# A hybrid attention, S5 and RG-LRU step: score and gate products over 128 rows, sample PV in two runs

## The chip, the cores and the metric

The kernel runs on one core of a Trainium2 chip. The metric is device time in microseconds of one execution. TensorE (PE in the profile) multiplies matrices into PSUM; VectorE (DVE), ScalarE (ACT) and GpSimd (POOL) do the elementwise work; SyncE (SP) issues most of the DMAs.

## The reference

One layer over a prompt of 2048 tokens and eight sample sequences of 4 tokens each (2080 token columns), in f32. `proj = x @ w_in` (1024 to 6400 columns) is split into queries, keys, values, gates and the inputs of three branches:

- attention with a window of 128 keys, 8 query heads of 64 in 2 groups of keys and values, a relative bias and a sink per head: `scores = q k^T / 8 + bias`, softmax with the sink in the denominator, times v. The sample sequences attend to 128 cached keys and their own.
- S5, a diagonal complex state space with a GELU and a gated output.
- RG-LRU: `r = sigmoid(x_block @ w_a + b_a)`, `i = sigmoid(x_block @ w_x + b_x)` for eight blocks of 64, then a linear recurrence.

Each branch is multiplied by its gate and by its `w_branch`; the three are merged with sigmoid gates, multiplied by `w_out`, added to the scaled input and normalised. The states and caches are returned too.

## The kernel before

Products are made accurate by splitting a number into a high part, which the fast matmul type float32r holds, and a low part. `mm3` (lines 98 to 101) adds three matmuls: high by high, high weights by low input, low weights by high input.

The first phase is `x @ w_in`: 48 column tiles of 128, each over five token units of 512, 512, 512, 272 and 272 columns (`gemm`, 24 matmuls a unit). Side streams for S5, its GLU, RG-LRU and attention are Python generators; `tick` counts the columns issued so far and takes a step of the current stream after so many, so the order of all instructions is fixed when the program is built. The second phase multiplies the three branches (`y_unit`), the third is `w_out` and the layer norm.

Units of the gate tiles are evacuated by one ScalarE and two VectorE operations (L89, L104, L233), the other units of attention's time by ScalarE alone.

RG-LRU (`lru_stream`): 4 column blocks by 5 chunks (512, 512, 512, 284, 284 columns). `f_split` makes for each half g a tile `f` whose own 64 rows hold that half's high part and whose other 64 rows its low part. Four matmuls a chunk write the PSUM tile `sa`: high weights by all 128 rows of `f` (L887), then low weights by the own 64 rows (L890). The weights `lru_w` stand in both halves of the rows.

Attention (`attn_stream`): 16 blocks of 128 queries, two groups, so 32 scores. `score(n)` has eight matmuls in four pairs:

```python
PE.matmul(o, hi.rearrange("p i t -> p (i t)"), kk[kv][:, keys], start=True, stop=False)
PE.matmul(o, lo.rearrange("p i t -> p (i t)"), kl[rows, keys], start=False, stop=True)
```

The first (L1024) has queries with high and low parts stacked over 128 rows, against the keys' high part in both halves; the second (L1025) the queries' high part, 64 rows, against the keys' low part `kl`. Columns are 192 (64 and 128 in block 0). An iteration n issues `score(n)`, the copies of the next block's queries and keys (`prep`), PV of score n-2 (`pvm`, L1099), the four transposes of the weights of score n-1 (`ptr`, L1051), VectorE's addition of the bias and the maximum (L1039 on), and, after 2.5 units of x @ w_in, the exponentials (ScalarE, L89) and the normalisation (VectorE, L1008 to L1010). The transposes of the next iteration need the last of these. `vtr` transposes a block's values (L982) from the tile `vr`.

The sample sequences come after the prompt's attention. Their PV (L1227, L1228) has for each of eight sequences a product over 128 cached rows and one over 4 new rows, plain f32, each of which shows as two matmuls in the trace.

Of the kernel before, what the change touches and what calls it, by code (L numbers as in the profile page):

```python
# [27 lines left out]
# how much of x @ w_in runs between the steps of a side stream  # L28
# [5 lines left out]
# column tiles of w_in in the order of the first phase  # L34
# [19 lines left out]
def kernel(ctx: ExitStack, tc: tile.TileContext, I, O):  # L54
# [81 lines left out]
    # ------------------------------------------------------------ side streams  # L136
    # A stream yields how much of x @ w_in its engines need before its next step.
# [19 lines left out]
    # ------------------------------------------------------------ weight stream  # L157
# [25 lines left out]
    # ------------------------------------------------------------ evacuations of the first phase  # L183
# [52 lines left out]
    # ------------------------------------------------------------ S5  # L236
    def s5_stream():
# [18 lines left out]
        # relative bias along the distance, for the attention's table  # L256
# [70 lines left out]
        # powers of the transition, 0..8  # L327
# [16 lines left out]
        # input matrix  # L344
# [24 lines left out]
        # per group with real over imaginary: powers for the output kernel, and the fourth for the samples  # L369
# [10 lines left out]
        # decay over eight steps and its unit phase, whose powers undo the rotation  # L380
# [61 lines left out]
        # lag kernels, with d at lag nought  # L442
# [217 lines left out]
        # final states  # L660
# [15 lines left out]
    # ------------------------------------------------------------ S5: GELU and GLU  # L676
# [73 lines left out]
    # ------------------------------------------------------------ RG-LRU  # L750
# [6 lines left out]
    def lru_stream():  # L757
# [9 lines left out]
        # log sigmoid  # L767
# [49 lines left out]
        def x_in(i, c):  # L817
            """Inputs of a chunk with the three before; the samples follow with their own."""
            t0, n = LUN[c]
            x = p.tile([128, 516], FT, name=uid("lx"), tag="lx", bufs=2)  # L820
            if c == 0:
                G.memset(x[:, 0:3], 0.0)
                SD.dma_start(x[:, 3:3 + n], xD[i][:, :n])
            else:
                m = min(t0 + n, TP) - t0 + 3
                SD.dma_start(x[:, :m], xD[i][:, t0 - 3:t0 - 3 + m])
            if c == 4:
                SD.dma_start(O["conv_p"][:, i], x[:, 228:231])
                smp = x[:, 231:287].rearrange("p (b s) -> p b s", s=7)
                V.tensor_copy(smp[:, :, 0:3], c0[:, i])  # L830
                SD.dma_start(smp[:, :, 3:7], xD[i][:, TP:T].rearrange("p (b t) -> p b t", t=4))
                SD.dma_start(O["conv_s"][:, i], smp[:, :, 4:7])
            cin[i, c] = x
# [19 lines left out]
        def f_split(j):  # L853
            """A block's values with high and low parts stacked; its own half is high."""
            if j >= len(chunks):
                return
            i, c = chunks[j]
            t0, n = LUN[c]
            o = xfs[i][:, t0:t0 + n]
            fs = [p.tile([128, 512], FR, name=uid("f"), tag=f"f{g}")[:, :n] for g in range(2)]  # L860
            for g in range(2):
                own, oth = half(g)
                act(fs[g][own], o[own], AF.Copy)
                V.tensor_sub(fs[g][oth], o[own], fs[g][own])
            return fs
# [15 lines left out]
        for i in range(4):  # L881
            wh, wl = wt
            R = big("R")
            for c, (t0, n) in enumerate(LUN):
                ps = sa()
                for g in range(2):
                    PE.matmul(ps[:, g, :n], wh[:, g], cur[g], start=True, stop=False)  # L887
                for g in range(2):
                    own = half(g)[0]
                    PE.matmul(ps[:, g, :n], wl[own, g], cur[g][own], start=False, stop=True)  # L890
                cur = f_split(i * 5 + c + 1)
                xf = xfs[i]
                ig = p.tile([128, 512], FT, name=uid("ig"), tag="ig")
                for g in range(2):
                    own, oth = half(g)
                    act(R[own, t0:t0 + n], ps[own, g, :n], AF.Tanh, scale=0.5, bias=hba[own, i:i + 1])
                    act(ig[own, :n], ps[oth, g, :n], AF.Tanh, scale=0.5, bias=hbx[oth, i:i + 1])
                stt(xf[:, t0:t0 + n], ig[:, :n], 1.0, xf[:, t0:t0 + n], OP.add, OP.mult)
                conv(i * 5 + c + 2)
                if c == 2 and i + 1 < 4:  # L900
                    wt = w_prep(i + 1)
                    w_in_(i + 2)
                yield
            b_ = xf
            aa = big("a")
            act(aa, R, AF.Exp, scale=c2[:, i:i + 1], bias=c2[:, i:i + 1])
            yield
            act(R, R, AF.Tanh, scale=nc2[:, i:i + 1], bias=nc2[:, i:i + 1])
            yield
            act(R, R, AF.Sqrt)  # L910
            stt(R, aa, 1.0, R, OP.add, OP.mult)
            stt(b_, b_, 0.5, R, OP.mult, OP.mult)
            V.memset(aa[:, 2048:2104].rearrange("p (b s) -> p b s", s=7)[:, :, 2], 0.0)
            V.tensor_copy(b_[:, 2048:2104].rearrange("p (b s) -> p b s", s=7)[:, :, 2], l0[:, i])
            V.tensor_tensor_scan(R, aa, b_, 0.0, op0=OP.mult, op1=OP.add)
            hs = p.tile([128, 8, 4], FT, name=uid("hs"), tag="hs", bufs=2)
            V.tensor_copy(hs, R[:, 2048:2104].rearrange("p (b s) -> p b s", s=7)[:, :, 3:7])
            SD.dma_start(hD[i][:, :TP], R[:, :TP])
            SD.dma_start(hD[i][:, TP:T], hs.rearrange("p b t -> p (b t)"))
            SD.dma_start(O["lru_p"][:, i:i + 1], R[:, 2047:2048])  # L920
            SD.dma_start(O["lru_s"][:, i], hs[:, :, 3])
            yield
            if i + 1 < 4:
                yield
        es.close()

    # ------------------------------------------------------------ attention
    def attn_stream():
# [5 lines left out]
        # Partitions hold 64 queries of two heads: the first or the second half of a block, with the 192 keys  # L934
        # that this half may see. A query's bias runs over the same distances in either half.
# [5 lines left out]
        raw, QK, ST_, VN = {}, {}, {}, {}  # L941

# [3 lines left out]
        def load(b):  # L946
# [5 lines left out]
            v = w([128, 128], "vr", bufs=3)  # L952
# [3 lines left out]
        def prep(b):  # L956
            q, k, v = raw.pop(b)
            k0 = 0 if b else 128
            # a group's queries with high and low parts stacked, its keys' high part twice; the group's own half is high
            qs = [w([128, 2, 4, 64], f"q{g}", FR) for g in range(2)]  # L960
            kk = [w([128, 256], f"k{g}", FR) for g in range(2)]
            kl = w([128, 256], "kl", FR)
# [6 lines left out]
            QK[b] = (qs, kk, kl, v)  # L969

            def low():
                for g in range(2):
# [3 lines left out]
                    V.tensor_sub(kl[own, k0:], k[own, k0:], kk[g][own, k0:])  # L976
# [3 lines left out]
        def vtr(b):  # L980
            ps = psum.tile([128, 512], FT, name=uid("mm"), tag="mm", bufs=3)
            PE.transpose(ps[:, 0:128], QK[b][3], ident)  # L982
# [3 lines left out]
            # the rows' halves as they are, the first twice, the second twice, swapped  # L986
# [8 lines left out]
        def soft_max(P, m, nh, sinks_ap):  # L995
            """P: scores [128, nh, n], replaced by the weights of the softmax; m: its sums."""
# [15 lines left out]
        def score(n):  # L1012
            b, kv = divmod(n, 2)
            qs, kk, kl, _ = QK[b]
            rows = slice(kv * 64, kv * 64 + 64)
# [3 lines left out]
            for h in range(2):  # L1019
                keys = slice(64 * h + k0[h], 64 * h + 192)  # L1020
                for i in range(2):
                    o = pv[:, h, i, k0[h]:]
                    hi, lo = qs[kv][:, h, 2 * i:2 * i + 2], qs[kv][rows, h, 2 * i:2 * i + 2]
                    PE.matmul(o, hi.rearrange("p i t -> p (i t)"), kk[kv][:, keys], start=True, stop=False)  # L1024
                    PE.matmul(o, lo.rearrange("p i t -> p (i t)"), kl[rows, keys], start=False, stop=True)  # L1025
# [6 lines left out]
            def front():  # L1032
# [7 lines left out]
                # of the outer 64 keys on either side, a query sees each in one block only  # L1040
# [107 lines left out]
        # ---- the sample group: all sequences at once, keys of the others left out  # L1148
# [25 lines left out]
        # cache rows that stay, then the new rows behind them  # L1174
# [50 lines left out]
        for b_ in range(8):  # L1225
            c = slice(b_ * 16, b_ * 16 + 16)
            PE.matmul(pv[:, :, b_], vc[:, b_], PT[:, :, c], start=True, stop=False)  # L1227
            PE.matmul(pv[:, :, b_], vnn[:, b_], PN[:, :, c], start=False, stop=True)  # L1228
# [8 lines left out]
    # ------------------------------------------------------------ first phase: x @ w_in  # L1237
# [41 lines left out]
    # ------------------------------------------------------------ inputs of the second phase  # L1279
# [56 lines left out]
    def seam(ti, u):  # L1336
        """Steps among the last units of the first phase that bring the second one's first inputs."""
# [83 lines left out]
    # ------------------------------------------------------------ second phase: branches, token units inside  # L1421
# [50 lines left out]
    def out_mm(t):  # L1472
# [4 lines left out]
        # the last tile in narrower column groups, whose statistics run while the next one is formed  # L1477
# [40 lines left out]
    # branch units; the next branch's inputs follow the last use of their place  # L1518
# [145 lines left out]
```

## Time and profile before

| | us |
|---|---|
| three runs | 1840.19, 1844.46, 1844.7 |
| median | 1844.46 |
| profiled execution: span | 1842.3 |
| TensorE busy | 1826.7 (99%) |
| TensorE weight loads busy | 1563.8 (85%) |
| VectorE busy | 1130.6 (61%) |
| ScalarE busy | 654.9 (36%) |
| GpSimd busy | 167.5 (9%) |

Of the profiled execution the page gives its span, from the first to the last instruction; what a run takes beside it is not listed apart. Busy times are shares of that span. Records of TensorE overlap, because a matmul is still running when the next one starts, so a mean duration is not a price: the distance between starts is. The granted clock is 1.00 at 2.4 GHz and 0.50 at 1.2 GHz.

### The profile page before, as it was taken

The numbers are of one execution on the slowest core, as the hardware profiler recorded it, in microseconds if no ns is written. First come the engines' busy times: TensorE is split into PE (matmuls) and PEld (weight loads), VectorE is DVE, ScalarE is ACT, GpSimd is POOL, SyncE is SP. The second block draws the span as 40 slices with busy tenths as digits, with TensorE's granted clock in tenths as the row PEclk, the third lists the DMA queues.
The fourth block names the chain that finished last, engine by engine and source line by source line (L and its number), as shares of the span: only waits on it lengthen the run. The fifth ranks groups of instructions, "written<-read, shape, count | busy, mean of one in ns | idle before, by whom it ended". The sixth has DMA issues, their size and how long they took to land. (4 is left out here: it accounts for less than half of the span.)

```text
span 1842.3 us, 26628 instructions
## 1 busy us (share of the span) xinstructions
PE 1826.7 (99%) x9788; PEld 1563.8 (85%) x9788; DVE 1130.6 (61%) x2450; ACT 654.9 (36%) x1382; POOL 167.5 (9%) x375
## 2 busy tenths in 40 slices
PE   8999999999999999999999999999999999999998
PEld 7888888888899888888888888888888888888886
DVE  5765888884343565544666788744343567666666
ACT  6213344432433466764455555411220202111110
POOL 0000000000000000000345454500000000000000
PEclk9999999999999999999999999999999999999999
DMA  7443343343333344343322334353454646542222
GB/s 229 111 130 102 115 115 106 108 114 109 113 112 100 95 124 108 92 102 103 96 79 75 104 105 124 101 164 97 140 171 140 195 131 197 181 147 91 92 91 75
DMA packets 214038, 220.36 MB, mean 120 GB/s; under 512 B 89124, under 2 KB 156708, under 8 KB 212740
## 3 DMA queue, kind: packets, MB, share of 16 engines
q1 hardware_dynamic: 182532, 169.27, 32.3%
q10 hardware_dynamic: 31376, 49.39, 7.5%
q8 instruction: 77, 1.26, 0.3%
q14 instruction: 53, 0.43, 0.1%
HBM read 136.53 MB, written 83.14 MB: 119 GB/s over the span
## 5 line engine op out<-in xcount | busy, mean ns | idle before, releaser
L99 PE MATMUL mm<-xh,wh 128*128 128x512 f32 (+1 forms) x1920 | 681.2, 355 | 0.0
L101 PE MATMUL mm<-xh,wl 128*128 128x512 f32 (+1 forms) x1920 | 673.8, 351 | 0.0
L100 PE MATMUL mm<-xl,wh 128*128 128x512 f32 (+1 forms) x1920 | 671.8, 350 | 0.0
L99 PEld LDWEIGHTS mm<-xh,wh 128*128 128x128 f32 x1920 | 362.0, 189 | 47.4 <-issue 2.9
L101 PEld LDWEIGHTS mm<-xh,wl 128*128 128x128 f32 x1920 | 361.6, 188 | 46.9 <-DVE wl L94 0.3
L100 PEld LDWEIGHTS mm<-xl,wh 128*128 128x128 f32 x1920 | 362.2, 189 | 42.2
L99 PE MATMUL py<-ah,wbh 128*128 128x512 f32 (+1 forms) x480 | 169.0, 352 | 1.2 <-DVE acc L104 1.2
L101 PE MATMUL py<-ah,wbl 128*128 128x512 f32 (+1 forms) x480 | 168.9, 352 | 0.0
L100 PE MATMUL py<-ah,wbh 128*128 128x512 f32 (+1 forms) x480 | 168.8, 352 | 0.0
L89 ACT ACTIVATE st<-mm 128x512 f32<-128x512 f32 (+1 forms) x170 | 86.9, 511 | 168.1 <-PE mm L101 154.5
L99 PEld LDWEIGHTS py<-ah,wbh 128*128 128x128 f32 x480 | 90.2, 188 | 14.6 <-issue 1.6
L100 PEld LDWEIGHTS py<-ah,wbh 128*128 128x128 f32 x480 | 90.3, 188 | 12.8
L101 PEld LDWEIGHTS py<-ah,wbl 128*128 128x128 f32 x480 | 90.2, 188 | 12.5
L1488 PE MATMUL po<-woh,mh 128*128 128x512 f32 x224 | 88.8, 396 | 0.0
L1490 PE MATMUL po<-woh,ml 128*128 128x512 f32 x224 | 88.8, 396 | 0.0
L1489 PE MATMUL po<-wol,mh 128*128 128x512 f32 x224 | 88.8, 396 | 0.0
L94 DVE TENSOR_TENSOR wl<-wr,wh 128x1024 fp32r<-128x1024 f32 x48 | 59.3, 1236 | 40.9 <-ACT wh L89 40.9
L104 DVE SCALAR_TENSOR_TENSOR gt<-gt,mm 128x512 f32<-128x512 f32 (+1 forms) x60 | 35.0, 584 | 72.5 <-ACT gt L89 72.3
L104 DVE SCALAR_TENSOR_TENSOR br<-br,py 128x512 f32<-128x512 f32 (+1 forms) x80 | 46.8, 585 | 50.9 <-PE py L101 43.7
L89 ACT ACTIVATE gt<-mm 128x512 f32<-128x512 f32 (+1 forms) x60 | 30.9, 516 | 120.6 <-PE mm L101 120.2
L89 ACT ACTIVATE wbh<-wbr 128x512 fp32r<-128x512 f32 x24 | 15.1, 629 | 148.0 <-PE py L100 117.3
L89 ACT ACTIVATE wh<-wr 128x1024 fp32r<-128x1024 f32 x48 | 50.5, 1051 | 23.7 <-DMA wr<-in_w_in_dram 10.0
(346 smaller groups left out, 2761.9 us busy)
## 6 DMA issues: line engine op xcount, KB each, us to landing
wr<-in_w_in_dram SPq DMA_DIRECT2D x48, 512.0 KB
mD<-st ACTq DMA_DIRECT2D x72, 256.0 KB
br<-mD SPq DMA_DIRECT2D x71, 256.0 KB
lx<-in_xr_dram SPq DMA_DIRECT2D x16, 512.0 KB
mD<-st ACTq DMA_DIRECT2D x48, 136.0 KB
br<-mD SPq DMA_DIRECT2D x47, 136.0 KB
xr<-in_xT_dram SPq DMA_DIRECT2D x24, 256.0 KB
wbr<-in_w_br_dram SPq DMA_DIRECT2D x24, 256.0 KB
```

Of the source, the lines that this page charges most:

```text
L89: return A.activation(out, in_, func, bias=bias, scale=scale, **kw)
L94: V.tensor_sub(lo, src, hi)
L99: PE.matmul(ps, wh, xh, start=start, stop=False)
L100: PE.matmul(ps, wh, xl, start=False, stop=False)
L101: PE.matmul(ps, wl, xh, start=False, stop=stop)
L104: return (eng or V).scalar_tensor_tensor(out, a, s, b, op0=op0, op1=op1)
L1488: PE.matmul(ps[c], h[:, k, :rows], wh, start=k == 0, stop=False)
L1489: PE.matmul(ps[c], h[:, k, :rows], wl, start=False, stop=False)
L1490: PE.matmul(ps[c], l[:, k, :rows], wh, start=False, stop=k == 7)
```

## The change

In RG-LRU the low weights are multiplied by all 128 rows of `f` instead of its own 64. In attention the keys' low part gets a tile for each group, whose other 64 rows are set to nought once, and the second product of a pair uses the same 128-row queries as the first. The value tile `vr` has two places instead of three. The sample PV issues the eight 128-row products first and then the eight 4-row ones, all into one PSUM bank, with one start and one stop. Comments were taken out, which shifts lines by a few.

```diff
                 for g in range(2):
-                    own = half(g)[0]
-                    PE.matmul(ps[:, g, :n], wl[own, g], cur[g][own], start=False, stop=True)
+                    PE.matmul(ps[:, g, :n], wl[:, g], cur[g], start=False, stop=True)
...
+        kl = [p.tile([128, 256], FR, name=f"kl{g}") for g in range(2)]
+        for g in range(2):
+            G.memset(kl[g][half(g)[1]].bitcast(FT), 0.0)
...
-            v = w([128, 128], "vr", bufs=3)
+            v = w([128, 128], "vr", bufs=2)
...
-            kl = w([128, 256], "kl", FR)
...
-            QK[b] = (qs, kk, kl, v)
+            QK[b] = (qs, kk, v)
...
-                    V.tensor_sub(kl[own, k0:], k[own, k0:], kk[g][own, k0:])
+                    V.tensor_sub(kl[g][own, k0:], k[own, k0:], kk[g][own, k0:])
...
-                    hi, lo = qs[kv][:, h, 2 * i:2 * i + 2], qs[kv][rows, h, 2 * i:2 * i + 2]
-                    PE.matmul(o, hi.rearrange("p i t -> p (i t)"), kk[kv][:, keys], start=True, stop=False)
-                    PE.matmul(o, lo.rearrange("p i t -> p (i t)"), kl[rows, keys], start=False, stop=True)
+                    qq = qs[kv][:, h, 2 * i:2 * i + 2].rearrange("p i t -> p (i t)")
+                    PE.matmul(o, qq, kk[kv][:, keys], start=True, stop=False)
+                    PE.matmul(o, qq, kl[kv][:, keys], start=False, stop=True)
...
         for b_ in range(8):
             c = slice(b_ * 16, b_ * 16 + 16)
-            PE.matmul(pv[:, :, b_], vc[:, b_], PT[:, :, c], start=True, stop=False)
-            PE.matmul(pv[:, :, b_], vnn[:, b_], PN[:, :, c], start=False, stop=True)
+            PE.matmul(pv[:, :, b_], vc[:, b_], PT[:, :, c], start=b_ == 0, stop=False, skip_group_check=True)
+        for b_ in range(8):
+            c = slice(b_ * 16, b_ * 16 + 16)
+            PE.matmul(pv[:, :, b_], vnn[:, b_], PN[:, :, c], start=False, stop=b_ == 7, skip_group_check=True)
```

## Rows read from the trace of the kernel before

**Rows 1.** The page's busy time of each engine (share of the span), with its instructions.

```profile
PE 1826.7 (99%) x9788; PEld 1563.8 (85%) x9788; DVE 1130.6 (61%) x2450; ACT 654.9 (36%) x1382; POOL 167.5 (9%) x375
```

**Rows 2.** Waits of TensorE, whole span: total us, times, longest; first and last.

```profile
PE mm L99 <- ACT xh L89: 4.9, 1, 4.9
...
PE mm L100 <- DVE xl L94: 0.2, 1, 0.2
```

**Rows 3.** Timeline of TensorE, an RG-LRU chunk of 512 columns: start, us, instruction.

```profile
627.04 0.40 PE L101 MATMUL mm<-xh,wl 128*128 128x512 f32 x1
627.27 0.63 PE L887 MATMUL sa<-f,lwh 128*128 128x512 f32 x2
...
628.59 0.40 PE L100 MATMUL mm<-xl,wh 128*128 128x512 f32 x1
```

**Rows 4.** Timeline of TensorE, a score and the PV behind it.

```profile
990.45 0.25 PE L1024 MATMUL sa<-k,q 128*128 128x192 f32 x1
990.63 0.35 PE L1025 MATMUL sa<-kl,q 64*128 64x192 f32 x1
990.91 0.36 PE L1024 MATMUL sa<-k,q 128*128 128x192 f32 x1
...
992.85 0.28 PE L1099 MATMUL sb<-ptl,vn 128*128 128x256 f32 x1
992.96 0.28 PE L1099 MATMUL sb<-ptq,vn 128*128 128x256 f32 x1
```

**Rows 5.** Timeline of TensorE: four transposes of a score, and that of block 13's values.

```profile
1128.92 0.60 PE L1051 MATMUL sc<-ident,S 128*128 128x128 f32 x4
...
1132.39 0.27 PE L982 MATMUL mm<-ident,vr 128*128 128x128 f32 x1
```

**Rows 6.** Timeline of TensorE's weight loads, in the score of rows 4.

```profile
990.91 0.19 PEld L1024 LDWEIGHTS sa<-k,q 128*128 128x128 f32 x1
...
992.85 0.19 PEld L1099 LDWEIGHTS sb<-ptq,vn 128*128 128x128 f32 x1
```

**Rows 7.** Groups by line and shape: busy us, mean ns, idle before.

```profile
L890 PE MATMUL sa<-f,lwl 64*128 64x512 f32 x24 | 6.0, 496 | 0.0
```

**Rows 8.** Timeline of TensorE, an RG-LRU chunk of 284 columns.

```profile
646.19 0.43 PE L887 MATMUL sa<-f,lwh 128*128 128x284 f32 x2
...
647.21 0.40 PE L100 MATMUL mm<-xl,wh 128*128 128x512 f32 x1
```

**Rows 9.** Timeline of TensorE, the sample PV and x @ w_in behind it.

```profile
1274.43 0.31 PE L1227 MATMUL sc<-PT,vc 128*128 128x32 f32 x2
...
1275.00 0.41 PE L1227 MATMUL sc<-PT,vc 128*128 128x32 f32 x2
...
1275.67 0.41 PE L1227 MATMUL sc<-PT,vc 128*128 128x32 f32 x2
...
1281.43 0.63 PE L100 MATMUL mm<-xl,wh 128*128 128x512 f32 x1
...
1284.84 0.40 PE L99 MATMUL mm<-xh,wh 128*128 128x512 f32 x1
```

**Rows 10.** Stretches: length, busy us (instructions) of each engine, granted clock, DMA.

```profile
1278.04:1284.84 6.80, 6.80 (x20) 5.62 (x20) 1.23 (x1) 1.60 (x3) 0.00 (x0) 0.50 0.06 10
...
876.45:1043.17 166.72, 166.72 (x888) 138.24 (x887) 112.52 (x245) 88.33 (x270) 77.58 (x154) 1.00 0.27 86
1043.17:1178.39 135.22, 135.22 (x723) 112.18 (x721) 113.83 (x239) 69.12 (x217) 66.11 (x129) 1.00 0.36 111
```

**Rows 11.** Timeline of GpSimd, its first work in attention, with the idle time before.

```profile
864.39 0.61 POOL L989 CAST vn<-vn 64x512 fp32r<-64x512 f32 x1 [116.30 <-DMA mD<-st]
```

**Rows 12.** Timeline of SyncE's queue: the load of block 15's values.

```profile
1146.76 0.38 SPq L953 DMA_DIRECT2D vr<-vD  x1
```

**Rows 13.** Waits of VectorE from 876 to 1043, then 1043 to 1178 us.

```profile
DVE S L1039 <- PE sa L1025: 36.6, 16, 3.9
...
DVE S L1039 <- PE sa L1025: 10.0, 7, 2.2
```

**Rows 14.** Timeline of VectorE, the normalisation before the transposes of rows 5.

```profile
1127.25 0.69 DVE L1010 TENSOR_TENSOR S<-S,m 128x512 f32<-128x512 f32 x1
```

More of the change, by code (lines that the diff above doesn't have):

```diff
@@ L981, in vtr @@
             ps = psum.tile([128, 512], FT, name=uid("mm"), tag="mm", bufs=3)
-            PE.transpose(ps[:, 0:128], QK[b][3], ident)
+            PE.transpose(ps[:, 0:128], QK[b][2], ident)
             h = w([128, 4, 2, 2, 64], "vn", FR, 3)
@@ L1013, in score @@
             b, kv = divmod(n, 2)
-            qs, kk, kl, _ = QK[b]
-            rows = slice(kv * 64, kv * 64 + 64)
+            qs, kk, _ = QK[b]
             ps = sa()
```

## Prediction

> **What bounds the kernel now.** The page comes first. TensorE is busy for 1826.7 of 1842.3 us, 99% of the span, and VectorE for 61% [rows 1]. The waits of TensorE come next: the first and the last of the five rows are 4.9 and 0.2 us, and the five add to 7.5 us [rows 2]. So nearly everywhere the next matmul is there when the one before it lets it in, and a matmul that lets its successor in sooner shortens the kernel by as much, until another engine is late. Busy time can't show this, since matmuls overlap in the records: what counts is the distance from one start to the next. That is read in the timeline.
>
> There the reader sees three prices. A 128-row matmul follows one of 512 columns by 0.23 us, 627.04 to 627.27 [rows 3], and in the prompt's PV one of 256 columns by 0.11 to 0.12 us, 992.85 to 992.96 [rows 4]. The four 128-column transposes behind PV stand 0.11 us apart: together they take 0.60 us, a single one 0.27 [rows 5]. But in a score, where 128-row and 64-row matmuls of 192 columns alternate, starts are 0.28 us apart, 990.63 to 990.91 [rows 4]. The weight loads tell why: normally a load runs under the matmul before its own, as the one at 992.85, whose matmul starts at 992.96; in the score the load of 990.91 begins only when the records start its own matmul, 990.91 as well [rows 4, 6]. A change in the number of rows keeps the load from being taken ahead, both going to 64 rows and coming back.
>
> **The change part by part.**
>
> *Score.* The low product now runs over 128 rows, the other group's 64 rows of the keys' low part being nought. Count and columns stay: eight matmuls a score, 32 scores. Between the first score matmul (990.45) and the second PV matmul behind it (992.85) lie 2.40 us [rows 4]; the 30 scores of blocks 1 to 15 all have 2.38 to 2.39 by unrounded starts. After the change this stretch is eight steps of a 192-column matmul and one of a 256-column one. No row shows 192 columns at 128 rows without a change of rows; the bounds are the transposes' 0.109 (128 columns) and PV's 0.120 (256). I take 0.113, as 192 lies between and the small one is already no cheaper. So 8 x 0.113 + 0.12 = 1.02, and the gain is 2.385 - 1.02 = 1.363 us (1.30 to 1.40). Thirty give 40.9. The two scores of block 0 alternate in the same way with 64 and 128 columns; they are taken at 1.0 each, an estimate between nothing and the 1.36 of the others: 2.0 in all. **Score: 42.9 us (41 to 44).**
>
> *RG-LRU gates.* Twenty chunks of two 128-row products and two 64-row ones; the latter become 128-row. The two 64-row ones use opposite halves of the rows and do run together: the 24 of 512 columns, of 496 ns each, cover only 6.0 us [rows 7]. With 512 columns the chunk takes 1.32 us from its first matmul to the second behind it (627.27 to 628.59) [rows 3]; five steps of 0.23 are 1.15: 0.17 gained, twelve times. With 284 columns it takes 1.02 us (646.19 to 647.21) [rows 8]; four steps of 0.13, which is 0.12 for 256 columns scaled up, and one of 0.23 are 0.75: 0.27, eight times. **Gates: 2.0 + 2.2 = 4.2 us (3.5 to 4.5).**
>
> A rule of the Trainium skill speaks against this edit. The page TensorEngine Tiling (Array Packing), sections Theoretical Speedup and Key Properties, says that products of at most 64 rows can be packed side by side for up to twice the speed, and also that changing the tiling mode drains the engine. The first half is what the pair shows; by it alone the edit would cost the lost overlap, 12 x 0.23 + 8 x 0.13 = 3.8 us, and the sum of the three parts would fall by 8.0. The second half is what the steps around the pair show, and by it the sum stands.
>
> *Sample PV.* Eight pairs of a 128-row and a 4-row product, each of two recorded matmuls, become two runs: sixteen changes of rows become two. At the clock's upper level a pair of products takes 0.67 us, 1275.00 to 1275.67, and first matmul to second behind is 7.00 us, 1274.43 to 1281.43 [rows 9]. But the granted clock fell to 0.50, 1.2 GHz, from 1278.04 to 1284.84 [rows 10], in the middle of these sparse matmuls, and the matmuls of x @ w_in behind them went at 0.43 instead of 0.23: eight of them to 1284.84, 1.6 us lost. At full clock the old order would have taken 8 x 0.67 + 0.3 = 5.7 us; the new one takes 31 steps of 0.11, and some 0.1 + 0.2 + 0.3 for the change to four rows, back, and the first load behind: 4.0. If the clock falls as before, 1.6 us are gained; if it stays up, 7.0 + 1.6 - 4.0 = 4.6. Whether it falls in 4 us of such work no row says; I take the middle. **Sample PV: 3 us (1.6 to 4.6).**
>
> *The rest at nothing.* Two memsets of 64x256 zeros on GpSimd when attention begins: it stood idle for 116.30 us before its first work there [rows 11], longer than any memset in the trace; without that cover they would delay the first score by under 1 us, the 0.61 of the 64x512 copy in that row. The keys' low part was one place for all blocks and stays so, as one place per group; the subtraction that writes it waits, as now, for the score that read it. The value buffer goes from three places to two. So the load of a block waits for the transpose two blocks back: that of block 13 starts at 1132.39, and block 15's load is issued at 1146.76 [rows 5, 12]. If it did wait, SyncE's queue would stand, with the weights of x @ w_in behind it; 14 us of cover exclude it.
>
> *What is late next.* The products given back, 50.1 us, are TensorE's alone; the other engines keep their work and get less time. VectorE is the one to watch. From 876 to 1043 us (x @ w_in evacuated by ScalarE) it is busy for 112.5 of 166.7 us and waits 36.6 us for score products; 16 scores take 21.8 us away, which fits. From 1043 to 1178, where x @ w_in's gate columns put two VectorE operations on every unit, it is busy for 113.8 of 135.2 us and its waits for score products are only 10.0 us [rows 10, 13]. Thirteen scores take 13 x 1.363 = 17.7 us away; 10.0 of that can come out of those waits, so up to 7.7 us don't fit unless other gaps close. Being late shows at the transposes of the weights of the softmax, which need VectorE's last operation: in the tightest place it ends at 1127.94 and the first transpose starts at 1128.92 [rows 5, 14], 0.98 us, less than the 1.36 that the score before it loses. Bounds: nothing (113.8 would just fit into 117.5) and 7.7. I take **4 us given back**, the middle.
>
> **The sum.** 42.9 + 4.2 + 3.0 - 4.0 = 46.1 us. The page gives the profiled execution's span, 1842.3; the three runs are 1840.2 to 1844.7 with a median of 1844.5, so what lies around the span is counted as 2.2 us and stays. 1844.5 - 46.1 = **1798 us**.
>
> **Rivals.**
> *VectorE takes over.* In the gate stage all 7.7 us are given back, and the earlier stage adds some 2 us, an estimate, where its transposes come as close; the sample PV's clock falls again. 50.1 - 1.4 - 9.7 = 39: 1805. For it: the 0.98 us [rows 5, 14]. Against: lateness can be carried a little past the stage's end.
> *All of it hidden.* VectorE's gaps close, and the clock stays up: 42.9 + 4.2 + 4.6 = 51.7: 1793.
> *No gain from the rows.* The 0.28 us might come from accumulating pairs on one place of PSUM, not from the rows, and then the edit does nothing: 1844. Against: PV's groups of three and x @ w_in's of 24 accumulate at 0.12 and 0.23 [rows 3, 4].
> *Slower.* Then, too, the gates' pair loses its overlap, and nothing comes back: 3.8 us, 1848. It decides if a score gains less than 3.8/32 = 0.12 us, that is if a step stays above 0.27. This is the packing rule above; against it, a chunk with its overlap takes 1.32 us where five steps without any would take 1.15 [rows 3].
>
> **How the numbers follow.** Chances: the forecast 0.62 (1795 to 1802), VectorE takes over 0.18, all hidden 0.13, no gain 0.04, slower 0.03. The range for 8 in 10 takes in both middle rivals: below, 51.7 with the score at its best (1.1 more) and a run as far under the median as the lowest shown (4.3), partly: 1790; above, 1805 with the score at its worst (1.9) and some 2 us of spread: 1809. A difference of 0.3%, 5.5 us, is about what a measurement of this kernel tells from no change. Faster by more: 0.93; within: 0.04; slower: 0.03.
>
> **What would show it.** Right: score matmuls 0.11 apart with loads that start under the matmul before; chunks of 1.15 and 0.75 us; the 16 sample matmuls 0.11 apart. VectorE's waits for score products from about 1020 us on (1043 less what is gained by then) nearly gone, and waits of TensorE's transposes for VectorE of some 4 us in all, a new row. Wrong: if steps stay near 0.28, the rows weren't the cause; if these waits, or waits for ScalarE, exceed 10 us, VectorE sets the pace there; and if the clock falls anywhere else, each us at 0.50 costs half a us.

## Result and the profile after

The changed kernel takes 1802.2 us (median; 1800.3 to 1804.9) against 1844.3: a ratio of 0.9777, with a 95% interval of 0.9764 to 0.9789. The forecast was 1798, the range 1790 to 1809. The profiled execution took 1802.31 us with a span of 1800.6, so 1.7 us lie around a span; spans are compared below, and theirs differ by 1842.3 - 1800.6 = 41.7 us. (The first phase has 50 column tiles, not the 48 named above: two of them are loaded at the very start. No number rests on it.)

The page's busy times:

```profile
PE 1777.6 (99%) x9788; PEld 1548.2 (86%) x9788; DVE 1130.1 (63%) x2450; ACT 654.4 (36%) x1382; POOL 167.9 (9%) x377
```

There are as many matmuls and as many VectorE instructions as in [rows 1]: TensorE needs 49 us less for its own, VectorE as long as before; GpSimd has the two memsets more. Busy TensorE is still 99%, so that view alone doesn't tell where the time went. The timeline of TensorE in a score does, and under it that of the weight loads in the same stretch:

```profile
987.92 0.25 PE L1025 MATMUL sa<-k,q 128*128 128x192 f32 x1
988.01 0.28 PE L1026 MATMUL sa<-kl,q 128*128 128x192 f32 x1
988.13 0.27 PE L1025 MATMUL sa<-k,q 128*128 128x192 f32 x1
988.24 0.27 PE L1026 MATMUL sa<-kl,q 128*128 128x192 f32 x1
...
988.80 0.30 PE L1100 MATMUL sb<-pth,vn 128*128 128x256 f32 x1
988.94 0.28 PE L1100 MATMUL sb<-ptl,vn 128*128 128x256 f32 x1
```

```profile
988.04 0.19 PEld L1025 LDWEIGHTS sa<-k,q 128*128 128x128 f32 x1
988.15 0.19 PEld L1026 LDWEIGHTS sa<-kl,q 128*128 128x128 f32 x1
```

Starts are 0.11 us apart instead of 0.28 [rows 4], and the load of the matmul at 988.13 begins at 988.04, under the one before it, where in [rows 6] it began with its own. From the first score matmul to the second PV matmul are 1.02 us here (1.01 in nearly all) instead of 2.40. The RG-LRU chunk of 512 columns and one of 284, TensorE's timeline again:

```profile
626.96 0.63 PE L887 MATMUL sa<-f,lwh 128*128 128x512 f32 x2
...
628.12 0.40 PE L100 MATMUL mm<-xl,wh 128*128 128x512 f32 x1
```

```profile
651.62 0.43 PE L887 MATMUL sa<-f,lwh 128*128 128x284 f32 x2
...
652.38 0.40 PE L100 MATMUL mm<-xl,wh 128*128 128x512 f32 x1
```

These are 1.16 and 0.76 us, against 1.32 [rows 3] and 1.02 [rows 8]. The sample PV, in the same view:

```profile
1236.96 1.87 PE L1228 MATMUL sc<-PT,vc 128*128 128x32 f32 x16
1238.76 1.97 PE L1231 MATMUL sc<-PN,vnn 4*128 4x32 f32 x16
1240.65 0.50 PE L99 MATMUL mm<-xh,wh 128*128 128x512 f32 x1
1240.99 0.39 PE L100 MATMUL mm<-xl,wh 128*128 128x512 f32 x1
```

Sixteen matmuls take 1.8 us; first to second behind is 4.03 us instead of 7.00 [rows 9], and in this profile the clock stayed up, so that x @ w_in behind it went at 0.23 at once.

By these prices the change should have brought 41.2 us in 30 scores, 2.1 in the two of block 0, 3.9 in the gates, and 3.0 + 1.6 in the sample PV: 51.8. The span fell by 41.7, so 10.1 us are missing. The view of stretches says where (length, then busy time and instructions of each engine, then TensorE's granted clock and the DMA); the first is the third to the eighteenth score, the second the 13 that follow, in the stage of the gate tiles:

```profile
869.89:1015.28 145.39, 145.05 (x889) 129.86 (x887) 112.07 (x245) 88.39 (x270) 77.63 (x154) 1.00 0.32 99
1015.28:1138.25 122.97, 119.23 (x722) 105.58 (x721) 112.59 (x238) 68.39 (x217) 65.62 (x128) 1.00 0.40 121
```

The first lost 166.72 - 145.39 = 21.3 us [rows 10], where 16 scores at 1.37 make 22.0: nearly nothing came back. The second lost 135.22 - 122.97 = 12.2 us, where 13 scores make 17.9: 5.6 came back. From there to the sample PV it is 1236.96 - 1138.25 = 98.7 us, where it was 96.0 [rows 9, 10] with one slow score more: 4.0 came back. Some 0.7 came back ahead of attention, where a gate product waited 0.7 us for ScalarE, and 0.4 behind the sample PV: 11.4 in all. Against that stand 1.3 us that the prices leave out. In the profile of before the granted clock was at 0.50 behind the first score:

```profile
858.20:861.61 3.41, 3.41 (x13) 3.12 (x14) 2.22 (x8) 1.41 (x6) 0.00 (x0) 0.50 0.91 257
```

In the changed kernel's profile it stayed up there, and x @ w_in between the two scores of block 0 took 7.32 us instead of 8.65. So the 10.1 are 11.4 us given back, less 1.3 of the clock.

TensorE's waits, whole span (total us, times, longest):

```profile
PE mm L99 <- ACT xh L89: 5.4, 1, 5.4
PE sc L1052 <- DVE S L1012: 2.7, 5, 1.1
PE sb L1100 <- POOL ptl L1082: 1.8, 3, 1.2
PE py L99 <- DVE acc L104: 1.3, 1, 1.3
PE sa L1025 <- ACT k L89: 0.9, 1, 0.9
PE sa L887 <- ACT ig L89: 0.7, 1, 0.7
PE sc L1052 <- ACT oo L89: 0.7, 1, 0.7
PE sb L1100 <- POOL pth L1082: 0.7, 1, 0.7
PE sa L1026 <- DVE kl L978: 0.4, 1, 0.4
```

In [rows 2] there were five rows and 7.5 us; here nine and 14.6. New are the transposes' wait for VectorE's normalisation, which the prediction named, and PV's wait for GpSimd's selections, which it did not. The waits understate the loss, since the end of a pipelined matmul is modelled: in the gate stage, from 1015 to 1138 us, they make some 3.7 us, where it gave back 5.6. Behind the stage PV waits twice for GpSimd, and then the clock falls (TensorE's timeline, and the stretch in the view of stretches):

```profile
1148.01 0.39 PE L1100 MATMUL sb<-pth,vn 128*128 128x256 f32 x1 [0.70 <-POOL pth L1082]
1149.58 0.39 PE L1100 MATMUL sb<-ptl,vn 128*128 128x256 f32 x1 [1.19 <-POOL ptl L1082]
```

```profile
1150.30:1153.72 3.42, 3.42 (x13) 2.83 (x12) 1.37 (x2) 1.19 (x2) 1.22 (x3) 0.50 0.37 68
```

3.42 us at 0.50 cost about 1.7 us, half of the stretch; with the waits of 0.70 and 1.19 that is 3.6 of the 4.0. VectorE's waits for score products, from 870 to 1015 us:

```profile
DVE S L1040 <- PE sa L1026: 15.2, 12, 2.5
```

36.6 us [rows 13] less 15.2 are 21.4: in the earlier stage VectorE gave up just what the scores took away. In the gate stage, where there were 10.0, the view has no such row any more.

### The profile page after: what moved, and what is told of

Its sections match the earlier page's. It is cut to its first block, busy times and chain, and to the rows that moved or that the text cites. A ratio compares the mean times of both kernels' runs of the same rounds, so it can differ in the third digit from the quotient of the medians.

```text
span 1800.6 us, 26639 instructions
## 1 busy us (share of the span) xinstructions
PE 1777.6 (99%) x9788; PEld 1548.2 (86%) x9788; DVE 1130.1 (63%) x2450; ACT 654.4 (36%) x1382; POOL 167.9 (9%) x377
```

## Experiments

The theory: a change of the number of rows between matmuls keeps the next weight load from running ahead, and what is saved is given back only where VectorE's load no longer fits. The rivals: another cause of the slow steps (accumulating pairs, 64 rows as such), and another cause of the give-back (GpSimd, fixed latencies). All ratios are against the kernel before.

**e1, the new tiles alone.** The `kl` tiles, their memsets and `bufs=2` as in the change; the product stays

```diff
-PE.matmul(o, lo.rearrange("p i t -> p (i t)"), kl[rows, keys], start=False, stop=True)
+PE.matmul(o, lo.rearrange("p i t -> p (i t)"), kl[kv][rows, keys], start=False, stop=True)
```

> The kernel before with only the new tiles: a tile of the keys' low part for each group with its memset, and two places for the values instead of three; all matmuls as before, the low ones over 64 rows. Theory (these cost nothing, they have cover): 1844 us, within 2 us of before, steps in a score still 0.28 us apart. Rival (the memset, the tile's place or the shorter buffer costs a wait that the change's result already contains): 1848 or more, with a new wait of TensorE or of SyncE's queue.

1844.3 us, ratio 1.0002 (0.9993 to 1.0011). These edits cost nothing, as the theory has it.

**e2, the score edit alone**, on e1:

```diff
-PE.matmul(o, lo.rearrange("p i t -> p (i t)"), kl[kv][rows, keys], start=False, stop=True)
+PE.matmul(o, hi.rearrange("p i t -> p (i t)"), kl[kv][:, keys], start=False, stop=True)
```

> The kernel before with the score edit alone (tiles as in e1, low products over 128 rows). Theory (a change of the number of rows costs about 0.17 us a step): 30 x 1.37 + 2 = 43 us less, minus about 8 us that other engines give back in and behind the gate stage, so 1809 us (1805 to 1812); steps 0.11 us apart. Rival (the pairs' accumulation on one place of PSUM is the cost): 1844 us, steps 0.28 apart.

1809.4 us, ratio 0.9812 (0.9799 to 0.9825): 34 us of the change's 42. Its waits for VectorE (2.8 us) and GpSimd (1.8 and 0.8) are those of the whole change, so the give-back belongs to this edit. The accumulating pairs are still there, in the same places of PSUM: that rival falls.

**e3, the RG-LRU edit alone** (the first hunk of the change).

> The kernel before with the RG-LRU edit alone. Theory (changes of rows cost more than the packed pair saves): chunks of 1.17 us instead of 1.32 and of 0.76 instead of 1.02, together 4 us less: 1840 us. Rival (the packing rule: the pair's overlap is lost and nothing comes back): 3.8 us more, 1848 us.

1839.8 us, ratio 0.9973 (0.9963 to 0.9984): 5 us by the ratio, 3.7 by the medians, and chunks as in the change. The pair's overlap was lost and the kernel still got faster. The Trainium skill (TensorEngine Tiling (Array Packing), Theoretical Speedup) offers up to twice the speed for products packed side by side; for a pair that stands alone this trace shows no gain, 1.32 us a chunk against 1.16 without it. The Trainium skill also says, on the same page under Key Properties, that changing the tiling mode drains the engine; the cost of the steps around the pair fits that, though a drain itself is not to be seen in a trace whose matmul ends are modelled.

**e4, the sample PV's order alone** (the last hunk).

> The kernel before with the sample PV's new order alone. Theory (changes of rows, and a clock that no longer falls there): the stretch from the first matmul to the second behind is 4.0 us instead of 7.0, and the matmuls of x @ w_in behind it go at 0.23 us: 4.6 us less, 1840 us. Rival (the clock falls in this order as well, and its not falling in the changed kernel was the moment): the granted clock of the stretch is 0.50 again, and 1.6 us less: 1843 us.

1841.4 us, ratio 0.9990 (0.9981 to 0.9999): 2 us, neither of the two numbers. The view of stretches of its profile, the PV and what follows it:

```profile
1272.54:1276.58 4.04, 4.04 (x34) 3.91 (x33) 0.00 (x0) 0.23 (x1) 0.00 (x0) 1.00 0.31 97
1276.65:1279.90 3.25, 3.25 (x9) 2.58 (x8) 1.23 (x1) 1.31 (x2) 0.00 (x0) 0.50 0.13 20
```

The stretch is 4.04 us, as forecast, but the clock fell right behind it. So the new order doesn't rule a fall out, and that the clock stayed up in the changed kernel's profile was luck of that execution.

**e5, the score's 64-row products grouped**, on the kernel before:

```diff
+for h in range(2):
+    keys = slice(64 * h + k0[h], 64 * h + 192)
+    for i in range(2):
+        hi = qs[kv][:, h, 2 * i:2 * i + 2].rearrange("p i t -> p (i t)")
+        PE.matmul(pv[:, h, i, k0[h]:], hi, kk[kv][:, keys], start=i == 0, stop=False, skip_group_check=True)
+for h in range(2):
+    keys = slice(64 * h + k0[h], 64 * h + 192)
+    for i in range(2):
+        lo = qs[kv][rows, h, 2 * i:2 * i + 2].rearrange("p i t -> p (i t)")
+        PE.matmul(pv[:, h, i, k0[h]:], lo, kl[rows, keys], start=False, stop=i == 1, skip_group_check=True)
```

> The kernel before with the score's eight matmuls in another order alone: the four high products (128 rows) first, then the four low ones, still over 64 rows; one change of rows instead of seven inside a score. Theory (the change of rows is what costs): the four high ones 0.11 us apart, the four low ones close together as well, and only two slow steps, into and out of the 64 rows: from the first score matmul to the second PV matmul behind it about 8 x 0.11 + 0.12 + 2 x 0.17 = 1.35 us instead of 2.39, which is 31 us less, minus some 4 given back: 1817 us (1813 to 1821). Rival A (accumulating pairs on one place of PSUM): the same as the change, since the pairs are parted: 1.01 us. Rival B (64 rows are slow in themselves, whatever stands ahead of them): the low ones stay 0.28 us apart, 1.9 us: about 1832 us.

1812.6 us, ratio 0.9832 (0.9817 to 0.9847). TensorE's timeline in one score:

```profile
994.71 0.59 PE L1023 MATMUL sa<-k,q 128*128 128x192 f32 x4
995.23 0.69 PE L1028 MATMUL sa<-kl,q 64*128 64x192 f32 x4
995.85 0.39 PE L1102 MATMUL sb<-pth,vn 128*128 128x256 f32 x1
996.07 0.28 PE L1102 MATMUL sb<-ptl,vn 128*128 128x256 f32 x1
```

1.36 us, where 1.35 were expected. Four 64-row matmuls take 0.69 us, the last of them 0.27 by its record: the fourth starts 0.42 us after the first, whose own load lies in that time, so about 0.11 apart once the first is loaded. So 64 rows are not slow, only the step into them and the one out of them. Rivals A (1.01) and B (1.9) both fall. An order alone, without any padding, brings nine tenths of e2; it is some 3 us behind e2.

**e6, less VectorE in the gate stage**, on the changed kernel:

```diff
-stt(gt, gt, 1.0, ps[:, :n], OP.add, OP.mult)
+if b == "a":
+    stt(gt, gt, 1.0, ps[:, :n], OP.add, OP.mult)
```

> The changed kernel, in which the gate units of branches c and b leave out VectorE's multiplication of the gate by its own input (one of two VectorE operations a unit; that part of the gate isn't computed). Theory (in the gate stage VectorE has too much to do in the shorter time, and TensorE's new waits for VectorE, GpSimd and ScalarE all stand behind it): the 5.6 us given back there and most of the 4.0 us behind it return: 1794 us (1792 to 1797). Rival (GpSimd's selections or a fixed chain of latencies set the pace, not VectorE's load): 1800 us or more, waits for GpSimd as before.

1794.8 us, ratio 0.9732 (0.9718 to 0.9747). The 13 scores of the gate stage (view of stretches), and TensorE's waits there and on to 1140 us:

```profile
1015.56:1133.53 117.97, 117.66 (x722) 105.34 (x721) 101.84 (x219) 68.68 (x217) 68.54 (x128) 1.00 0.42 127
```

```profile
PE sc L1053 <- DVE S L1013: 0.3, 1, 0.3
```

Without give-back the stage would take 135.2 - 17.9 = 117.3; it takes 118.0. With 10.8 us less VectorE work the stage's waits for GpSimd and ScalarE vanish too, with GpSimd as busy as before. What was taken away, the gate's multiplication, is no part of the chain from a score to its PV: it is VectorE's load that counts.

**e7, less GpSimd**, on the changed kernel:

```diff
-for x in (h, l):
-    block_before(x[lo, 0], x[lo, 0])
-    own_block(x[lo, 1], x[lo, 1])
```

> The changed kernel, in which GpSimd leaves out four of its eight selections a score (half of the mask isn't applied); VectorE's work stays. Theory (VectorE's load): TensorE's waits for the normalisation stay at 2 to 3 us, only those for GpSimd vanish, with the fall of the clock behind the last one: 1798 us (1796 to 1801). Rival (GpSimd): both kinds vanish, 1793 us.

1796.4 us, ratio 0.9740 (0.9725 to 0.9754), between the two numbers. Stretch and waits, as for e6:

```profile
1013.29:1133.84 120.55, 118.25 (x722) 105.36 (x721) 110.09 (x237) 68.18 (x216) 40.16 (x77) 1.00 0.41 123
```

```profile
PE sc L1052 <- DVE S L1012: 2.3, 4, 0.9
```

The waits for VectorE stay, as the theory said, and 3.2 us over the ideal stay with them; those for GpSimd go, and with them the fall of the clock behind the stage (here, and in e6, it fell at the sample PV instead). So GpSimd is not innocent: its selections start when VectorE has made the low part, and stand between VectorE and PV. The two engines are not quite parted by this run, though. VectorE's own operations got shorter too while GpSimd had less to do: between 1015 and 1134 us the 24 that make the queries' low part took 492 ns in the mean instead of 544, and the 12 that make the keys' low part 466 instead of 518, 1.9 us together. Either end of that chain can be eased; only easing VectorE clears all of it.

**e8, the gate stage's iterations further apart**, on the changed kernel:

```diff
-yield ATT_SCORE
+yield ATT_SCORE + (0.6 if n >= 17 else 0.0)
-yield ATT_SOFTMAX
+yield ATT_SOFTMAX + (0.6 if n >= 17 else 0.0)
```

> The changed kernel with attention's two steps an iteration 0.6 us of x @ w_in further apart each from iteration 17 on, so that the gate stage's iterations get 1.3 us more of TensorE's time; all work is done. Theory (VectorE's load in a too short time): the waits in the gate stage vanish, attention ends some 15 us later, and 6 to 9 us come back: 1795 us (1792 to 1798). Rival (fixed latencies, or the later end of attention collides with the gate tiles of branch a): 1800 us or more.

1801.5 us, ratio 0.9764 (0.9748 to 0.9780): no gain. TensorE's waits from 1013 to 1260 us, and the stretch from the sample PV on:

```profile
PE sc L1228 <- DVE PT L1221: 2.1, 1, 2.1
PE sb L1100 <- POOL ptl L1082: 0.6, 1, 0.6
PE mm L984 <- DVE gt L104: 0.4, 1, 0.4
```

```profile
1245.90:1256.00 10.10, 10.10 (x45) 9.97 (x46) 0.09 (x1) 0.54 (x2) 0.00 (x0) 0.50 0.12 34
```

The gate stage's waits went, as forecast; but the stream ran into the point by which the sample PV must be issued. Its steps came without x @ w_in between them, TensorE waited 2.1 us for VectorE's copy, and the clock was at 0.50 for 10.1 us, about 5 us lost.

**e9, the same with 0.25 in place of 0.6.**

> The changed kernel with 0.25 us of x @ w_in more at each of attention's two steps an iteration from iteration 17 on; all work is done. In e8 the gate stage's waits were gone, but 114 more matmuls of x @ w_in ahead of the sample PV pushed it against its deadline, 60 matmuls on, where its steps came without space. Theory (load in too short a time, and e8 lost its gain at the deadline): about 36 to 45 matmuls more, the deadline isn't reached, the gate stage's waits mostly vanish, 4 to 7 us come back: 1797 us (1795 to 1799). Rival (the waits are fixed latencies): 1801 to 1803 us.

1796.0 us, ratio 0.9743 (0.9730 to 0.9757): 6 us less than the change. The sample PV comes 33 matmuls of x @ w_in later, short of its deadline. TensorE's waits from 1014 to 1240 us:

```profile
PE sb L1100 <- POOL ptl L1082: 0.8, 2, 0.6
PE sc L1052 <- DVE S L1012: 0.6, 2, 0.4
```

With all work done, time alone clears most of it. More time helps a chain of fixed latencies as well as a load, so this run by itself doesn't tell the two apart; e6, which took load away and left the chain as it was, does.

**e10, the low part first**, on the changed kernel:

```diff
-for x in late:
+for x in reversed(late):
```

> The changed kernel with VectorE's two late steps swapped: the low part of the transposed weights, which GpSimd's selections wait for, ahead of the addition to the output; all work is done. If the chain from VectorE over GpSimd to PV is what is late (e6 and e7 each freed it), its waits, 2.5 us, and the fall of the clock behind the last one, 1.7 us, shrink: 1799 us (1797 to 1801). If VectorE's load alone counts, nothing changes: 1802 us.

1800.5 us, ratio 0.9769 (0.9756 to 0.9782), which isn't told apart from the change. In its profile the waits for GpSimd fell from 2.5 to 0.7 us and those for VectorE rose from 2.7 to 3.7: the lateness moved to the other path.

**e11, e9 and e10 together.**

> e9 and e10 together; all work is done. If either cures the same lateness, no better than the better one: 1796 us (1794 to 1798).

1794.0 us, ratio 0.9732 (0.9718 to 0.9745). The best with all work done; its interval overlaps e9's. From 1013 to 1240 us its profile has no wait of TensorE left.

**e12, the exponentials earlier**, on the changed kernel, `ATT_SCORE` 0.6 less and `ATT_SOFTMAX` 0.6 more from iteration 17 on.

> The changed kernel with the exponentials 0.6 us of x @ w_in nearer to their score from iteration 17 on and the next score that much further from them; the sum of both steps stays, all work is done. If the path score, maximum, exponentials, normalisation, transposes is what is late, its waits (2.7 us) shrink: 1799 us (1797 to 1801). If the load counts, nothing comes back, since the period stays: 1802 us; it may get worse where the exponentials then wait for the maximum and hold ScalarE's queue: 1804 us.

1803.8 us, ratio 0.9786 (0.9772 to 0.9799). Moving the softmax within an unchanged period brings nothing, as load would have it; but it also moved room from one step of the chain to the next, so a chain late in both would look the same.

## Why the prediction was right, and where its terms were off

*Score.* Right in mechanism and size: 1.374 us a score where 1.363 were worked out; e2 and e5 show the cause, and e5 the price: one change into 64 rows and one out of them cost 0.35 us together (1.36 against 1.01).

*Gates.* Right: 3.9 us for 4.2, alone 3.7 by the medians (e3).

*Sample PV.* The length was right (4.03 for 4.0). The 1.6 us of the clock were put half in and half out. Alone the edit brought 2 us (e4), in the change's profile 4.6, since there the clock stayed up; in most profiles with the new order it fell (last section), so 1.6 of the 4.6 are luck of that execution.

*The rest at nothing.* Right (e1).

*What is late next.* This term was mis-sized: 4 us were forecast, bounds 0 to 7.7, and 11.4 were given back, 10.1 of them left in the span's difference. Of this 5.6 lie in the gate stage, within the bounds; e6 shows that they are VectorE's load in the shorter time, and e9 that more time clears most of them. The 4.0 us behind the stage were missed: lateness was thought to be carried past the stage's end at no cost, but there PV waited for GpSimd, and a clock at 0.50 followed. The prediction looked at one path from VectorE to TensorE, over the normalisation; the other, over the low part and GpSimd's selections, has as little room: in e7, with half of the selections left out, its waits are gone. That the wait brought the clock down is not shown. In e2 PV waited as long at the same place (0.75 and 1.19 us), and from the end of its gate stage to the sample PV the clock stayed at 1.00:

```profile
1140.60:1237.76 97.16, 95.22 (x516) 81.16 (x514) 53.35 (x94) 19.01 (x45) 12.84 (x24) 1.00 0.52 138
```

These are 97.2 us against the changed kernel's 98.7, and the 1.5 between them are about what 3.42 us at 0.50 cost.

*The rival "VectorE takes over"* put 9.7 us back, near the 10.1, but by another way: 7.7 in the gate stage and 2 in the earlier one, where 5.6 and 0.7 were measured, and nothing behind them. It also had the clock fall in the sample PV and so came to 1805.

*The number.* The measured 1802.2 lies between that and the forecast, inside the range and just outside the forecast's own 1795 to 1802. That it came so near is in part luck: 6.1 us too little were given back in the sum, but its other terms were 1.7 too small (51.8 for 50.1), nearly all of it the clock at the sample PV, and 1.7 us lay around the span instead of 2.2. 1798.4 + 6.1 - 1.7 - 0.5 = 1802.3.

## What to carry to other kernels

Where matmuls of different row counts alternate, look at the distance between starts and at where each weight load begins: a load that starts with its own matmul shows a change that costs. Pad to one row count, or group by row count where padding costs memory (e5 gave nine tenths of e2's gain by order alone). And before counting a gain on a busy TensorE, add up what the next engine has to do in each stage's shorter time, along every path on which it feeds TensorE; where a stage is over-full, move the work to one that isn't (e9), with an eye on the next deadline (e8).

## What the runs showed of the hardware

A packed pair of 64-row matmuls, which does overlap, loses to two 128-row ones in a row if it stands alone between 128-row matmuls: 1.32 against 1.16 us with 512 columns. And the granted clock fell to 0.50 without an idle TensorE, in or right behind the 32 small matmuls of the sample PV. With the old order it did so in all five profiles: at 1278.04 us in the kernel before, 1280.45 in e1, 1242.19 in e2, 1273.33 in e3 and 1248.44 in e5. With the new order it fell in six of nine, e4, e6, e7, e11 and e12 without a wait before it and e8 behind one of 2.1 us, and not in the changed kernel's own profile nor in those of e9 and e10, whose sample PV took the same 4.03 us: the same instructions, a different clock.
